# Late transposes of a stage's last token tile, and one-column inverse-root steps as tensor-scalar operations, in an fp32 two-block transformer

## The chip, the cores and the metric

One NeuronCore of a Trainium2 chip runs one program. The metric is the device time of one execution in microseconds (us). The engines are TensorE (PE in the profile; PEld is its weight load), VectorE (DVE), ScalarE (ACT), GpSimd (POOL) and SyncE (SP, which issues most DMAs).

## What is computed

Two transformer blocks in fp32 on one sequence of 512 tokens of width 1024. The first block adds three gated branches (gated linear attention, attention over 128 selected keys, cross attention to 256 memory tokens). The second has layer A (mLSTM with memory attention, then a feed-forward part of width 2816) and layer B (sliding-window attention with memory attention, then a feed-forward part). Each sublayer ends and the next begins in the same way, and this is what the change is about:

```python
def rmsnorm_2(x, g):
    y = x * lax.rsqrt(jnp.mean(x * x, axis=-1, keepdims=True) + EPS)
    return y * g

def swiglu(h, w_in, w_out):
    gate, up = jnp.split(h @ w_in, 2, axis=-1)
    return (jax.nn.silu(gate) * up) @ w_out

x = x + rmsnorm_2(y @ w, g_post)     # end of a sublayer
h = rmsnorm_2(x, g_pre)              # start of the next one
```

## The kernel before

**Products.** An fp32 product is made exact enough from three passes: each operand is split into a high part (rounded by ACT) and a low part (the difference). `mm3` (L373 to L375) issues high x high, low x high and high x low into one PSUM bank. The 512 tokens are four token tiles of 128 rows. Weights are streamed as items of [128, 1024]: SP loads an item (`load_more`, L302), ACT makes the high part (L336), DVE or POOL the low part (L337, in two pieces of 512 columns). `ctl["lo"] = POOL` gives the low parts to POOL at the end of each sublayer and in the first units of the feed-forward part. Some weights are multiplied by a gain on POOL first (L310). In the names, `h_` and `l_` stand ahead of the weight's key: `ag0`, `au0` are gate and up item 0 of layer A's feed-forward part, `ay` its down weights, `bmk`, `bmv` the memory keys and values of layer B, `kvk`, `kvv` its shared keys and values.

**Memory.** Every large tile lies in a slot of 4 KB per partition. `get` takes the slot that has been free longest, `put` (and `drop`) returns one, so the order of frees decides which tile a load has to wait for. PSUM has two banks `mm`, three `a` and three `t`.

**End of a sublayer.** `close_sublayer` (for `wo`, `awo` and `bwo`) multiplies token tile after token tile by the output weights. For tile t it then runs `residual` (sum of squares on ACT L1106, z = y * gain L1107, inverse root, x update L1113) and `prenorm` (squares L1115, inverse root, hn L1130 or, without a gain, L1128). `to_T` transposes hn on PE (L497, 8 transposes) and evicts them as high part by ACT (L502) and low part by DVE (L503). The transposes of tile t - 1 stand behind the products of tile t, those of tile 3 in a fifth turn behind the loop, so that the next stage's products follow them in the program. A scheduler then orders each engine's instructions, so the code's order is not quite the order on the engines.

**Next stage.** Behind `awo` and `bwo` the feed-forward part starts with `units_half`: five items g0, u0, g1, u1, g2, first their products with tokens 0 to 255 (tiles 0 and 1), then with tokens 256 to 511 (tiles 2 and 3). A half item is 24 matmuls of 256 columns. Behind layer A's feed-forward part `mem_kv` makes keys (mk0, mk1) and values (mv) of the memory, which need no token tile, and then come kvk and kvv, which do.

**Inverse root.** `rsqrt` with one value per row (n = 1) is a chain of one-column DVE operations: the first guess L450, then L455, L462, L463, L455, L465, L466. All but L450 and L465 read two or three tensors of [128, 1]:

```python
V.scalar_tensor_tensor(t, y_, v, y_, op0=OP.mult, op1=OP.mult)                     # L455
V.scalar_tensor_tensor(t, t, -10.0 / 3.0, t, op0=OP.add, op1=OP.mult)              # L462
V.scalar_tensor_tensor(y, t, 5.0, g, op0=OP.add, op1=OP.mult)                      # L463
V.tensor_scalar(t, t, -0.5 * 0.375 ** 3, 1.5 * 0.375, op0=OP.mult, op1=OP.add)     # L465
V.tensor_tensor(y, y, t, op=OP.mult)                                               # L466
```

Of the kernel before, what the change touches and what calls it, by code (L numbers as in the profile page):

```python
# [20 lines left out]
D = 1024  # L21
# [8 lines left out]
# column offsets of w_in  # L30
# [76 lines left out]
    # ---- second block, layer A  # L107
# [8 lines left out]
    # ---- layer B  # L116
# [10 lines left out]
def pack_weights(inp):  # L127
    """lays the weight matrices out item after item, a partition's data in one run"""
# [26 lines left out]
# ---------------------------------------------------------------- constants (of shapes alone)  # L155
# [49 lines left out]
def model_kernel(ctx: ExitStack, tc: tile.TileContext, A, out):  # L205
# [11 lines left out]
    # ------------------------------------------------------------ memory: slots of 4 KB a partition  # L217
# [43 lines left out]
    # ------------------------------------------------------------ side streams  # L261
# [19 lines left out]
    # ------------------------------------------------------------ weights  # L281
# [89 lines left out]
    # ------------------------------------------------------------ products  # L371
# [5 lines left out]
    class Act:  # L377
        """transposed activations [feature, token] as exact high and low parts"""
# [25 lines left out]
    def unit_T(key, act, ntok=512):  # L404
        """128 columns, transposed: [128 columns, tokens]"""
# [21 lines left out]
    def units_N(key, act, nt, post, bank=ps_mm):  # L427
        """256 columns, token tile by token tile: [128 tokens, 256]"""
# [13 lines left out]
    # ------------------------------------------------------------ norms  # L442
    def rsqrt(ss, n, scale, name):
        """(ss * scale + EPS) ** -0.5; ss ** -0.5 without a scale"""
# [20 lines left out]
        V.tensor_scalar(t, t, -0.5 * 0.375 ** 3, 1.5 * 0.375, op0=OP.mult, op1=OP.add)  # L465
# [26 lines left out]
    def to_T(hn, act, tt, keep=False):  # L492
        """transposes the rows of token tile tt and splits them"""
        for j in range(2):
            pt = ps_t([128, 4, 128])
# [31 lines left out]
    def head_product(o, st, j, tk, kh, kl):  # L527
        """o = q k^T; kh, kl: high and low part of the keys, in both halves (kl: at least in half j)"""
# [19 lines left out]
    def add_max(dst, src, mask, first, mx):  # L548
        """dst = src + mask; mx = max(first, dst)"""
# [7 lines left out]
    # ============================================================ start  # L557
# [20 lines left out]
    # the memory tokens enter the products without their norm, which the results are scaled by  # L578
# [66 lines left out]
    # --- keys and values of the memory of block 1  # L645
# [25 lines left out]
    # --- index keys, index weights, low-rank gate input  # L671
# [19 lines left out]
    # --- GLA gates: cumulative log decay per chunk of 64 (before the 1/16), two heads a tile  # L691
# [35 lines left out]
    # --- index queries  # L727
# [6 lines left out]
    # --- the choice of the 128 keys with the largest scores  # L734
# [36 lines left out]
    # --- cross attention, head by head  # L771
# [38 lines left out]
    def silu_gate(z, src, scale, act, k):  # L810
        """act[k] = src * scale * z * (1 + tanh(z / 2)); z in PSUM"""
# [29 lines left out]
    # --- DSA operands  # L841
# [80 lines left out]
    # --- branches: merged += 2 sigmoid(gates) * (y @ w_out)  # L922
# [24 lines left out]
    # --- GLA operands  # L947
# [105 lines left out]
    # --- DSA output gate and branch  # L1053
# [10 lines left out]
    # --- GLA output gate and branch  # L1064
# [35 lines left out]
    def residual(y, t, g, cols=HALVES, more=True):  # L1100
        """x += rmsnorm(y) * g for token tile t; y: its banks"""
# [19 lines left out]
    def prenorm(t, sx, g):  # L1121
        """the normalised rows of token tile t; without g their gain is left to the weights"""
# [10 lines left out]
    def close_sublayer(key, act, gpost, g, a):  # L1133
        """x += rmsnorm(act^T @ w) * gpost, then the transposed normalised activations a of the next sublayer"""
# [3 lines left out]
        prev = None  # L1138
        for t in range(5):
            if t < 4:  # L1140
                cols = HALVES if t < 3 else LAST
                y = [(ps_a if t % 2 else ps_mm)() for _ in cols]
                for n, sl in enumerate(cols):
                    for k in range(8):
                        mm3(y[n][:, :sl.stop - sl.start], act.hi(k)[:, 128 * t:128 * t + 128], act.lo(k)[:, 128 * t:128 * t + 128],
                            ws[k].hi[:, 0, sl], ws[k].lo[:, 0, sl], k == 0, k == 7)
# [528 lines left out]
```

## Time and profile before

| | |
|---|---|
| time, median of 3 runs | 2102.74 us (2099.51 to 2103.94) |
| span of the profiled execution | 2097.9 us |
| PE busy in it | 2038.2 us, 97% |
| DVE, ACT, POOL busy | 1102.7, 810.8, 259.0 us |

The profiled execution has no time of its own beside its span; the span lies 4.8 us under the median of the runs. All times inside the program below are counted from the span's start.

### The profile page before, as it was taken

Reading aid. Unit: us, or ns where it says so; the run is one execution under the profiler, and the core shown is the slowest. Engines: PE = TensorE matmul, PEld = TensorE weight load, DVE = VectorE, ACT = ScalarE, POOL = GpSimd, SP = SyncE. Lnnn points to the kernel's source line nnn. Section 1 sums busy time; section 2 is a strip of 40 time slices with the busy share of each in tenths; the row PEclk is TensorE's granted clock in tenths of the full one; section 3 lists DMA queues with packets and bytes.
Section 4 is the critical chain, followed back from the end, with each engine's and each line's share of the span. In section 5 each row is a group of like instructions: output and inputs, shape, how many; then the busy total and the mean of one; then the engine's idle time right before and its main releaser. Section 6 shows DMA issues by size and latency. Waiting matters only on the chain.

```text
span 2097.9 us, 26836 instructions
## 1 busy us (share of the span) xinstructions
PE 2038.2 (97%) x10234; PEld 1686.3 (80%) x10234; DVE 1102.7 (53%) x2455; ACT 810.8 (39%) x1787; POOL 259.0 (12%) x211
## 2 busy tenths in 40 slices
PE   6999999999999999999998999999989989999998
PEld 6888778879777888898877888888876778888887
DVE  8744896354654343762677443342757774333423
ACT  4533443344423242453544333232435743223311
POOL 7201100000111111000022111102220031111000
PEclk9999999999999999999999999999999999999999
DMA  6321131222222243141124222244111232312421
GB/s 260 114 71 51 56 118 61 81 81 71 81 71 82 90 141 113 69 155 60 54 78 151 67 89 81 81 152 126 60 49 38 76 116 70 111 56 81 135 81 41
DMA packets 54528, 189.57 MB, mean 90 GB/s; under 512 B 6648, under 2 KB 8832, under 8 KB 54400
## 3 DMA queue, kind: packets, MB, share of 16 engines
q1 hardware_dynamic: 52640, 185.36, 26.8%
q0 software_dynamic: 464, 1.44, 0.3%
q8 instruction: 80, 1.31, 0.2%
q10 hardware_dynamic: 1296, 1.07, 0.2%
q14 instruction: 48, 0.39, 0.1%
HBM read 185.73 MB, written 2.11 MB: 90 GB/s over the span
## 4 chain that ended last, share of the span: by engine, by line
PE 90%; DVE 6%; issue 1%; ACT 1%; DMA 1%; SPq 0%; DVEq 0%; ACTq 0%
PE mm L373 21%; PE mm L375 21%; PE mm L374 21%; PE pa L373 4%; PE pa L375 4%; PE pa L374 4%; PE pa L530 2%; PE pt L375 1%; PE pt L373 1%; PE pt L374 1%; PE pa L529 1%; PE pt L497 1%; DVE rst L455 1%; PE pa L880 1%; PE pt L1432 1%
## 5 line engine op out<-in xcount | busy, mean ns | idle before, releaser
L509 POOL TENSOR_TENSOR ffal<-t,ffah 128x512 fp32r<-128x512 f32 x44 | 61.2, 1390 | 421.1 <-ACT ffah L508 421.1
L1250 DVE SCALAR_TENSOR_TENSOR t<-t,mm 128x512 f32<-128x512 f32 x42 | 28.8, 685 | 82.5 <-PE mm L375 82.5
L497 PE MATMUL pt<-ident,hn 128*128 128x128 f32 x192 | 31.7, 304 | 36.7 <-DVE hn L1130 20.3
L374 PE MATMUL mm<-hTl,h_au 128*128 128x512 f32 (+1 forms) x176 | 66.8, 379 | 0.0
L373 PE MATMUL mm<-hTh,h_au 128*128 128x512 f32 (+1 forms) x176 | 66.8, 379 | 0.0
L373 PE MATMUL mm<-hTh,h_bu 128*128 128x512 f32 (+1 forms) x176 | 66.8, 379 | 0.0
L374 PE MATMUL mm<-hTl,h_bu 128*128 128x512 f32 (+1 forms) x176 | 66.8, 379 | 0.0
L375 PE MATMUL mm<-hTh,l_au 128*128 128x512 f32 (+1 forms) x176 | 66.8, 379 | 0.0
L375 PE MATMUL mm<-hTh,l_bu 128*128 128x512 f32 (+1 forms) x176 | 66.8, 379 | 0.0
L373 PE MATMUL mm<-hTh,h_ag 128*128 128x512 f32 (+1 forms) x168 | 63.8, 380 | 0.0
L374 PE MATMUL mm<-hTl,h_ag 128*128 128x512 f32 (+1 forms) x168 | 63.8, 380 | 0.0
L375 PE MATMUL mm<-hTh,l_ag 128*128 128x512 f32 (+1 forms) x168 | 63.7, 379 | 0.0
L373 PE MATMUL mm<-hTh,h_bg 128*128 128x512 f32 (+1 forms) x168 | 63.7, 379 | 0.0
L374 PE MATMUL mm<-hTl,h_bg 128*128 128x512 f32 (+1 forms) x168 | 63.7, 379 | 0.0
L375 PE MATMUL mm<-hTh,l_bg 128*128 128x512 f32 (+1 forms) x168 | 63.6, 379 | 0.0
L1247 ACT ACTIVATE t<-mm 128x512 f32<-128x512 f32 x40 | 23.7, 593 | 95.7 <-PE mm L375 95.7
L497 PEld LDWEIGHTS pt<-ident,hn 128*128 128x128 f32 x192 | 24.0, 155 | 42.2 <-issue 29.1
L1248 DVE SCALAR_TENSOR_TENSOR t<-t,mm 128x512 f32<-128x512 f32 x40 | 27.3, 683 | 57.7 <-ACT t L1247 57.7
L508 ACT ACTIVATE ffah<-t 128x512 fp32r<-128x512 f32 x44 | 27.5, 624 | 73.7 <-DVE t L1250 73.6
L337 DVE TENSOR_TENSOR l_ay<-w_ay,h_ay 128x512 fp32r<-128x512 f32 x44 | 30.1, 731 | 45.5 <-ACT h_ay L336 33.9
L337 DVE TENSOR_TENSOR l_bu<-w_bu,h_bu 128x512 fp32r<-128x512 f32 x38 | 25.6, 690 | 49.2 <-PE mm L374 21.3
L337 DVE TENSOR_TENSOR l_by<-w_by,h_by 128x512 fp32r<-128x512 f32 x44 | 29.2, 712 | 37.0 <-ACT h_by L336 23.2
(943 smaller groups left out, 6596.3 us busy)
## 6 DMA issues: line engine op xcount, KB each, us to landing
w_ag<-in_wpk SPq DMA_DIRECT2D x22, 512.0 KB, 3.9
w_au<-in_wpk SPq DMA_DIRECT2D x22, 512.0 KB, 3.6
w_ay<-in_wpk SPq DMA_DIRECT2D x22, 512.0 KB, 3.7
w_bu<-in_wpk SPq DMA_DIRECT2D x22, 512.0 KB, 3.5
w_bg<-in_wpk SPq DMA_DIRECT2D x22, 512.0 KB, 3.6
w_by<-in_wpk SPq DMA_DIRECT2D x22, 512.0 KB, 3.6
x<-in_x SPq DMA_DIRECT2D x8, 512.0 KB, 6.4
w_mk<-in_wpk SPq DMA_DIRECT2D x8, 512.0 KB, 6.1
```

The source lines that it names most:

```text
L337: (ctl["lo"] or V).tensor_tensor(l, s, f(h), op=OP.subtract)
L373: PE.matmul(o, lh, rh, start=first, stop=False)
L374: PE.matmul(o, lh, rl, start=False, stop=False)
L375: PE.matmul(o, ll, rh, start=False, stop=last)
L455: V.scalar_tensor_tensor(t, y_, v, y_, op0=OP.mult, op1=OP.mult)
L497: PE.transpose(pt[:, k], hn[:, 512 * j + 128 * k:512 * j + 128 * k + 128], ident)
L508: ACT.activation(h, src, AF.Copy)
L509: POOL.tensor_tensor(l, src, f(h), op=OP.subtract)
L530: PE.matmul(o, st[64 * j:64 * j + 64, j, tk], kl[64 * j:64 * j + 64], start=False, stop=True)
L1247: ACT.activation(t, og, AF.Tanh, scale=0.5)
L1248: V.scalar_tensor_tensor(t, t, 1.0, og, op0=OP.add, op1=OP.mult)
L1250: V.scalar_tensor_tensor(t, t, 0.5, ou, op0=OP.mult, op1=OP.mult)
```

## The change

Three things are changed; lines that only lose a comment are left out. First, `close_sublayer` and `ffn` no longer issue the transposes of tile 3 (in `ffn`: tiles 2 and 3). They return them as a function `late`, which the next stage calls: `units_half` ahead of its last item's first half, `mem_kv` behind its first tile of values. Second, the down product of `ffn` takes its PSUM banks in another order and transposes each tile into the banks that held its products, and kvk is made as two whole items of 512 columns instead of two half items. Third, `rsqrt` with n = 1 and `sums` are written with tensor-scalar operations, whose second and third operands are per-row scalars.

```diff
     def rsqrt(ss, n, scale, name):
...
+        if n == 1:
+            t, t1, w, w1 = [sm(1, f"rs{c}") for c in "abcd"]
+            V.tensor_scalar(t, g, v, g, op0=OP.mult, op1=OP.mult)
+            V.tensor_scalar(t1, t, -10.0 / 3.0, t, op0=OP.add, op1=OP.mult)
+            V.tensor_scalar(y, t1, 5.0, g, op0=OP.add, op1=OP.mult)
+            V.tensor_scalar(w, y, v, y, op0=OP.mult, op1=OP.mult)
+            V.tensor_scalar(w1, w, a, b, op0=OP.mult, op1=OP.add)
+            r = sm(1, "rsr")
+            V.tensor_scalar(r, y, w1, None, op0=OP.mult)
+            return r
...
     def sums(s2, n):
...
-            V.scalar_tensor_tensor(v, s2[:, i:i + 1], 1.0 / D, u, op0=OP.mult, op1=OP.add)
+            V.tensor_scalar(v, s2[:, i:i + 1], 1.0 / D, u, op0=OP.mult, op1=OP.add)
...
-    def units_half(keys, act):
+    def units_half(keys, act, late):
...
             for c, o in zip(cs, os_):
+                if t == 0 and c is cs[-1]:
+                    late()
...
     def close_sublayer(key, act, gpost, g, a):
...
-        prev = None
-        for t in range(5):
-            if t < 4:
...
-            if prev is not None:
-                to_T(prev, a, t - 1)
-            if t < 4:
-                sx = residual(y, t, gpost, cols)
-                prev = prenorm(t, sx, g)
+        for t in range(4):
...
+            if t:
+                to_T(hn, a, t - 1)
+            sx = residual(y, t, gpost, cols)
+            hn = prenorm(t, sx, g)
             pump()
+        gpost.drop()
+        g.drop()
         ctl["lo"] = None
...
+        return lambda: to_T(hn, a, 3)
...
-    def mem_kv(a, p):
+    def mem_kv(a, p, late):
...
+        def keep_v(t, o):
+            ACT.activation(v[:, t], o, AF.Copy)
+            if t == 0:
+                late()
...
-        banks = [[ps_t(), ps_t()], [ps_t(), ps_a()], [ps_a(), ps_a()], [ps_mm(), ps_mm()]]
+        pools = [[ps_mm, ps_mm], [ps_a, ps_a], [ps_a, ps_t], [ps_t, ps_t]]
+        banks = [[f_() for f_ in fs] for fs in pools]
...
+            if more and t in (1, 2):
+                to_T(rows[t - 1], nxt, t - 1, bank=pools[t - 1])
...
+        def rest():
+            for t in (2, 3):
+                to_T(rows[t], nxt, t, bank=pools[t])
...
-    o0, o1 = units_half(["kvk0", "kvk1"], hB)
-    ACT.activation(kr[:, 0], o0, AF.Copy)
-    ACT.activation(kr[:, 1], o1, AF.Copy)
     for i in range(2):
+        o = unit_T(f"kvk{i}", hB)
+        ACT.activation(kr[:, i], o, AF.Copy)
         start(s_ropek(i))
```

The order on PE behind `awo`, of before: the transposes of tile 3 (`pt<-ident,hn`) stand among the first-half products of g1 (`h_ag_9687`).

```order
L373 MATMUL pa<-hTh,h_ag_9687 128x256
L374 MATMUL pa<-hTl,h_ag_9687 128x256
L497 MATMUL pt<-ident,hn 128x128 x4
L375 MATMUL pa<-hTh,l_ag_9688 128x256
L373 MATMUL pa<-hTh,h_ag_9687 128x256
L497 MATMUL pt<-ident,hn 128x128 x4
L374 MATMUL pa<-hTl,h_ag_9687 128x256
L375 MATMUL pa<-hTh,l_ag_9688 128x256
```

The same place after the change: the transposes stand between the last first-half product of u1 (`h_au_9797`) and the first one of g2 (`h_ag_9805`).

```order
L374 MATMUL pa<-hTl,h_au_9797 128x256
L375 MATMUL pa<-hTh,l_au_9798 128x256
L510 MATMUL pt<-ident,hn 128x128 x8
L373 MATMUL pa<-hTh,h_ag_9805 128x256
L374 MATMUL pa<-hTl,h_ag_9805 128x256
L375 MATMUL pa<-hTh,l_ag_9806 128x256
```

From the end of the sublayer's products on, 62 first-half matmuls stand ahead of the transposes before, and 96 after; behind the transposes, 24 first-half matmuls (all of g2) are left where there were 58. Behind `bwo` the same rows stand with layer B's weights.

The order on ACT at that place, of before: the high parts of tile 3's transposes (`hTh<-pt`, four of them, each of two contraction tiles) and the weights around them; `h_au_10160` belongs to item u5.

```order
L502 ACTIVATE hTh<-pt 128x2x128
L336 ACTIVATE h_ag_10052<-w_ag_9748 128x512
L502 ACTIVATE hTh<-pt 128x2x128
L336 ACTIVATE h_au_10088<-w_au_9778 128x512
L502 ACTIVATE hTh<-pt 128x2x128 x2
L336 ACTIVATE h_au_10088<-w_au_9778 128x512
L336 ACTIVATE h_ag_10124<-w_ag_10020 128x512 x2
L336 ACTIVATE h_au_10160<-w_au_10058 128x512 x2
```

After the change, `h_au_10280` is the high part of item u5:

```order
L336 ACTIVATE h_ag_10244<-w_ag_10140 128x512 x2
L515 ACTIVATE hTh<-pt 128x2x128 x2
L336 ACTIVATE h_au_10280<-w_au_10178 128x512 x2
L515 ACTIVATE hTh<-pt 128x2x128 x2
L1266 ACTIVATE t_10092<-mm 128x512
```

It now stands between the two pairs of tile 3's evictions. Its item is loaded into the slot of the pre-norm gain, which is free only when DVE has made hn of tile 3 (L1130 before); before, it went to the slot of z, which L1107 frees earlier.

The order on PE ahead of the shared keys of layer B, of before: tile 3's transposes stand in the first half of kvk1 (`h_kvk_12599`).

```order
L374 MATMUL mm<-hTl,h_kvk_12597 128x256
L375 MATMUL mm<-hTh,l_kvk_12598 128x256
L373 MATMUL mm<-hTh,h_kvk_12599 128x256
L497 MATMUL pt<-ident,hn 128x128 x8
L374 MATMUL mm<-hTl,h_kvk_12599 128x256
L375 MATMUL mm<-hTh,l_kvk_12600 128x256
```

After the change they stand inside the first tile of kvv (`h_kvv.0_12848`), behind mk0, mk1 and mv, and the first products of kvk over all 512 tokens follow them:

```order
L375 MATMUL pa<-h_kvv.0_12848,hTl 128x256
L373 MATMUL pa<-h_kvv.0_12848,hTh 128x256
L374 MATMUL pa<-l_kvv.0_12849,hTh 128x256
L510 MATMUL pt<-ident,hn 128x128 x8
L373 MATMUL mm<-hTh,h_kvk_12731 128x512
L373 MATMUL mm<-hTh,h_kvk_12733 128x512
L375 MATMUL pa<-h_kvv.0_12848,hTl 128x256
```

From the first product of mk0 on, 121 matmuls stood ahead of the transposes of tile 3, and now 107; tile 2's transposes stood behind 23 matmuls and stand behind 72.

## Rows read from the trace of the kernel before

**Rows 1.** Page, busy time (1) and chain that ended last (4).

```profile
PE 2038.2 (97%) x10234; PEld 1686.3 (80%) x10234; DVE 1102.7 (53%) x2455; ACT 810.8 (39%) x1787; POOL 259.0 (12%) x211
...
PE 90%; DVE 6%; issue 1%; ACT 1%; DMA 1%; SPq 0%; DVEq 0%; ACTq 0%
```

**Rows 2.** PE's waits: us in total, times, longest us.

```profile
PE pt L497 <- DVE hn L1130: 20.3, 3, 8.9
PE pt L497 <- DVE hn L1128: 7.9, 3, 5.3
PE pt L497 <- DVE hn L489: 7.9, 5, 3.9
...
PE mm L373 <- DVE rst L465: 2.7, 1, 2.7
```

**Rows 3.** Timeline of PE behind awo: start us, us, work [idle before].

```profile
1139.89 1.08 PE L497 MATMUL pt<-ident,hn 128*128 128x128 f32 x4 [8.93 <-DVE hn L1130]
```

**Rows 4.** Timeline of DVE behind awo, token tile 3.

```profile
1123.69 1.06 DVE L1094 SCALAR_TENSOR_TENSOR ssv<-ssy,ssv 128x1 f32<-128x1 f32 x1
...
1130.00 1.03 DVE L466 TENSOR_TENSOR rsy<-rsy,rst 128x1 f32<-128x1 f32 x1
1131.06 2.38 DVE L1113 SCALAR_TENSOR_TENSOR x<-z,rsy,x 128x512 f32<-128x512 f32 x2
...
1134.92 1.21 DVE L462 SCALAR_TENSOR_TENSOR rst<-rst 128x1 f32<-128x1 f32 x1
...
1138.99 1.41 DVE L1130 SCALAR_TENSOR_TENSOR hn<-x,rsy,gain 128x512 f32<-128x512 f32 x2
1140.33 1.29 DVE L337 TENSOR_TENSOR l_au<-w_au,h_au 128x512 fp32r<-128x512 f32 x2
```

**Rows 5.** Timeline of POOL behind awo.

```profile
1130.97 1.26 POOL L337 TENSOR_TENSOR l_au<-w_au,h_au 128x512 fp32r<-128x512 f32 x1
```

**Rows 6.** DVE operations by line: ns min/median/max, forms.

```profile
L463 DVE SCALAR_TENSOR_TENSOR rsy<-rst,rsi x54: 140/159/1191, 8.8 to 2092.8; 128x1 f32<-128x1 f32 x46, 128x4 f32<-128x4 f32 x8
...
L455 DVE SCALAR_TENSOR_TENSOR rst<-rsi,ssv x36: 203/219/1028, 861.3 to 2092.3; 128x1 f32<-128x1 f32 x36
...
L465 DVE TENSOR_SCALAR rst<-rst x54: 136/154/170, 9.4 to 2093.2; 128x1 f32<-128x1 f32 x46, 128x4 f32<-128x4 f32 x8
...
L449 DVE TENSOR_SCALAR rsv<-ssg x4: 157/567/971, 564.5 to 647.0; 128x4 f32<-128x4 f32 x4
```

**Rows 7.** Stretches behind awo: each engine's busy us, PEclk granted clock.

```profile
1135.00:1140.00 5.00, 0.11 (x1) 0.14 (x2) 4.83 (x7) 2.37 (x5) 3.56 (x3) 0.50 0.37 105
1140.00:1145.00 5.00, 5.00 (x24) 5.00 (x25) 4.24 (x10) 3.61 (x9) 0.00 (x0) 0.50 0.01 2
1145.00:1150.00 5.00, 5.00 (x43) 5.00 (x42) 2.40 (x4) 1.34 (x3) 0.00 (x0) 0.98 0.72 235
```

**Rows 8.** Page, DMA issues (6): KB each, us to landing.

```profile
w_au<-in_wpk SPq DMA_DIRECT2D x22, 512.0 KB, 3.6
```

**Rows 9.** Timelines ahead of layer B's keys: PE (first row) and DVE.

```profile
1526.42 2.29 PE L497 MATMUL pt<-ident,hn 128*128 128x128 f32 x8 [5.35 <-DVE hn L1128]
...
1516.19 0.88 DVE L455 SCALAR_TENSOR_TENSOR rst<-rsi,ssv 128x1 f32<-128x1 f32 x1
...
1523.59 0.99 DVE L466 TENSOR_TENSOR rsy<-rsy,rst 128x1 f32<-128x1 f32 x1
```

**Rows 10.** Timeline of DVE at the start of the program.

```profile
36.73 0.96 DVE L462 SCALAR_TENSOR_TENSOR rst<-rst 128x1 f32<-128x1 f32 x1
...
39.91 0.77 DVE L466 TENSOR_TENSOR rsy<-rsy,rst 128x1 f32<-128x1 f32 x1
```

**Rows 11.** Start of layer B's down product: PE (two rows) and DVE.

```profile
1970.70 0.39 PE L373 MATMUL pt<-h_by,ffah 128*128 128x512 f32 x1
...
1972.06 0.39 PE L373 MATMUL pt<-h_by,ffah 128*128 128x512 f32 x1
...
1972.48 0.68 DVE L1250 SCALAR_TENSOR_TENSOR t<-t,mm 128x512 f32<-128x512 f32 x1
```

More of the change, by code (lines that the diff above doesn't have):

```diff
@@ L464, in rsqrt @@
         vyy(y)
-        V.tensor_scalar(t, t, -0.5 * 0.375 ** 3, 1.5 * 0.375, op0=OP.mult, op1=OP.add)
+        V.tensor_scalar(t, t, a, b, op0=OP.mult, op1=OP.add)
         V.tensor_tensor(y, y, t, op=OP.mult)
@@ L490, in scaled, with to_T @@
         return hn
-    def to_T(hn, act, tt, keep=False):
+    def to_T(hn, act, tt, keep=False, bank=None):
         for j in range(2):
-            pt = ps_t([128, 4, 128])
+            pt = (bank[j] if bank else ps_t)([128, 4, 128])
             for k in range(4):
@@ L1137, in close_sublayer @@
         ctl["ahead"], ctl["lo"] = 1, POOL
-        prev = None
-        for t in range(5):
-            if t < 4:
[L1141 to L1146, printed above, removed]
-                tick(2)
-                if t == 3:
-                    drop(*ws)
-                    act.drop()
-                    ctl["ahead"], ctl["stage"] = 2, 3
-            if prev is not None:
-                to_T(prev, a, t - 1)
-            if t < 4:
-                sx = residual(y, t, gpost, cols)
-                prev = prenorm(t, sx, g)
+        for t in range(4):
+            cols = HALVES if t < 3 else LAST
+            y = [(ps_a if t % 2 else ps_mm)() for _ in cols]
+            for n, sl in enumerate(cols):
+                for k in range(8):
+                    mm3(y[n][:, :sl.stop - sl.start], act.hi(k)[:, 128 * t:128 * t + 128], act.lo(k)[:, 128 * t:128 * t + 128],
+                        ws[k].hi[:, 0, sl], ws[k].lo[:, 0, sl], k == 0, k == 7)
+            tick(2)
+            if t == 3:
+                drop(*ws)
+                act.drop()
+                ctl["ahead"], ctl["stage"] = 2, 3
+            if t:
+                to_T(hn, a, t - 1)
+            sx = residual(y, t, gpost, cols)
+            hn = prenorm(t, sx, g)
             pump()
+        gpost.drop()
+        g.drop()
         ctl["lo"] = None
+        return lambda: to_T(hn, a, 3)
     def mem_prep(l):
@@ L1187, in mem_kv @@
             pump()
-        units_N(f"{p}mv", a, 2, lambda t, o: ACT.activation(v[:, t], o, AF.Copy), ps_a)
+        def keep_v(t, o):
+            ACT.activation(v[:, t], o, AF.Copy)
+            if t == 0:
+                late()
+        units_N(f"{p}mv", a, 2, keep_v, ps_a)
         a.drop()
@@ L1235, in mem_block, with ffn @@
             put(*qs, *kv)
-    def ffn(p, l, hT, more, side={}):
+    def ffn(p, l, hT, late, more, side={}):
         gpost = Gain("g_ffn_post_2", l)
@@ L1241, in ffn @@
         ctl["lo"] = POOL
-        first = units_half([f"{p}g0", f"{p}u0", f"{p}g1", f"{p}u1", f"{p}g2"], hT)
+        first = units_half([f"{p}g0", f"{p}u0", f"{p}g1", f"{p}u1", f"{p}g2"], hT, late)
         ctl["lo"] = None
@@ L1277, in ffn @@
         nxt = Act(8, "hT") if more else None
-        prev = None
-        for t in range(5):
-            if t < 4:
-                for n in range(2):
-                    for k in range(NFF - NR, NFF):
-                        step(k, ws[k - NFF + NR], banks[t][n], t, HALVES[n])
-                tick(2)
-                if t == 3:
-                    drop(*ws)
-                    for j in range((NFF - NR) // 2, NFF // 2):
-                        act.drop_group(j)
-                    ctl["ahead"], ctl["stage"] = 2, 3
-            if prev is not None:
-                to_T(prev, nxt, t - 1)
-            if t < 4:
-                sx = residual(banks[t], t, gpost, more=more)
-                if more:
-                    prev = prenorm(t, sx, None)
+        rows = []
+        for t in range(4):
+            for n in range(2):
+                for k in range(NFF - NR, NFF):
+                    step(k, ws[k - NFF + NR], banks[t][n], t, HALVES[n])
+            tick(2)
+            if t == 3:
+                drop(*ws)
+                for j in range((NFF - NR) // 2, NFF // 2):
+                    act.drop_group(j)
+                ctl["ahead"], ctl["stage"] = 2, 3
+            if more and t in (1, 2):
+                to_T(rows[t - 1], nxt, t - 1, bank=pools[t - 1])
+            sx = residual(banks[t], t, gpost, more=more)
+            if more:
+                rows.append(prenorm(t, sx, None))
         gpost.drop()
         ctl["lo"] = None
-        return nxt
+        def rest():
+            for t in (2, 3):
+                to_T(rows[t], nxt, t, bank=pools[t])
+        return nxt, rest
     def wout(key, act, gpost, gnext):
-        gp, g, a = Gain(*gpost), Gain(*gnext), Act(8, "hT")
-        close_sublayer(key, act, gp, g, a)
-        gp.drop()
-        g.drop()
-        return a
+        a = Act(8, "hT")
+        return a, close_sublayer(key, act, Gain(*gpost), Gain(*gnext), a)
     memA = mem_prep(0)
-    hA = wout("wo", mg, ("g_post",), ("g_mix_pre_2", 0))
-    kvm = mem_kv(memA, "a")
+    hA, late = wout("wo", mg, ("g_post",), ("g_mix_pre_2", 0))
+    kvm = mem_kv(memA, "a", late)
     aux = get([32, 896], F32, "aux")
@@ L1475, in model_kernel @@
     put(*hm, *sgo)
-    hF = wout("awo", mix, ("g_mix_post_2", 0), ("g_ffn_pre_2", 0))
+    hF, late = wout("awo", mix, ("g_mix_post_2", 0), ("g_ffn_pre_2", 0))
     def rotary():
@@ L1506, in model_kernel @@
     sides_a = {6: lambda: T.update(rot=rotary()), 4: lambda: T.update(mem=mem_prep(1))}
-    hB = ffn("a", 0, hF, True, sides_a)
+    hB, late = ffn("a", 0, hF, late, True, sides_a)
     cosT, sinT = T["rot"]
     memB = T["mem"]
-    kvB = mem_kv(memB, "b")
+    kvB = mem_kv(memB, "b", late)
     def rope(dst, rawt):
@@ L1633, in model_kernel @@
     put(*khd, *kld, vB, T["rt"], *qx)
-    hF = wout("bwo", mix, ("g_mix_post_2", 1), ("g_ffn_pre_2", 1))
-    ffn("b", 1, hF, False)
+    hF, late = wout("bwo", mix, ("g_mix_post_2", 1), ("g_ffn_pre_2", 1))
+    ffn("b", 1, hF, late, False)
 def build(inputs):
```

8 lines of the change are left out of this document (3 added, 5 removed).

## The prediction

> **What bounds the kernel now.** The page comes first: PE is busy for 97% of the span, and the chain of work that ended last lies on PE for 90% and on DVE for 6% [rows 1]. So TensorE sets the time, and a gain can come only from places where it stands still or runs at a lower clock. The view of PE's waits lists these places [rows 2]. Nearly all are transposes of normalised rows that wait for DVE: three waits for hn from L1130 (20.3 us in all, the longest 8.9), three for hn from L1128 (7.9, the longest 5.3), five at the start of the program (7.9). One more of 2.7 us there is a product that waits for a DVE operation of a one-column inverse root.
>
> The timeline shows the longest one: behind `awo` PE stands still for 8.93 us until 1139.89, so from 1130.96 [rows 3]. The wait behind `bwo` reads the same, and the third one of L1130, behind `wo`, is then 20.3 - 2 x 8.93 = 2.4. On DVE the reason is visible [rows 4]: the one-column operations of token tile 3 take about 1 us each, as long as a small tile's work. Their own line shows minima of 0.14 and 0.20 us [rows 6]. In that stretch POOL makes low parts back to back until 1132.2 [rows 5]. It is the operations with two tensor inputs that stretch; L465, a tensor-scalar operation, never took over 0.17 us in its 54 uses [rows 6].
>
> The granted clock shows a second loss. During the wait it falls to 0.50, the lower level of 1.2 GHz, and stays there for the 5 us after it: 24 matmuls between 1140 and 1145, then 43 in the next 5 us [rows 7]. From 1139.89 to about 1145.1 PE does half of what it could, so each long wait costs about 2.6 us more. The two places together cost 2 x (8.93 + 2.6) = 23.1 us.
>
> **Late transposes behind awo and bwo.** 96 instead of 62 first-half matmuls now precede tile 3's transposes: 34 more, each 0.12 us (43 in 5 us) [rows 7], so 4.1 us. PE reaches the transposes at 1130.96 + 4.1 = 1135.1.
>
> Would hn be there? Between 1123.69 and 1131.03 six one-column operations took 1.06, 1.02, 0.67, 1.01, 0.99 and 1.03 us (first and last in [rows 4]), in place of 0.15 to 0.22 each: 4.7 us too much. In the second root three took 1.2 us (one of them in [rows 4]), 3.1 too much. As tensor-scalar operations I price all at the 0.15 of L465 plus 0.06 for a tensor's place, by the 0.22 of L455. The trace has no such operation with two per-row scalars; the bounds are 0.15 and the slow 1.0 of the old form, and I choose the low end because L465 stood in the same busy stretch. Then x starts at 1131.06 - 4.7 = 1126.4, takes 2.4 us beside POOL [rows 4], the squares and the second root need some 2.5, and DVE now does one item's low parts (1.3) ahead of hn, which takes 1.4 to 2.4. The first half of hn is ready at 1133 to 1135, the second by 1136. Of the wait, 0.4 us may stay. With it goes the low clock.
>
> Behind the transposes only g2's first half covers their eviction: 24 matmuls, 2.9 us. ACT evicts one pair, and must then make the high part of u5 before the second pair. u5's load starts when hn is finished (1134 to 1136), lands 3.6 us later [rows 8], ACT needs 1.1 for it and about 1 us for the eviction and its low part: 1139.7 to 1141.7. PE is back from transposes and g2 at 1135.1 + 1.0 + 2.9 = 1139.0 and uses the first pair for 0.7 us more: wait 0 to 2, and more if the load is slower. I take 1.7. Each place then saves 8.93 + 2.6 - 0.4 - 1.7 = 9.4, and both 18.8.
>
> **Behind layer A's feed-forward part.** Five one-column operations between 1516.19 and 1524.58 lasted 0.66 to 0.84 us too long, 3.9 in all (first and last in [rows 9]), and POOL was multiplying gains then. hn of tile 3 comes at 1522.5 instead of 1526.4. But PE now has 107 instead of 121 matmuls ahead of it, so it waits longer and has 14 x 0.12 = 1.7 us more to do behind. The long wait and its low clock stay. kvk now needs all tokens at once, so part of the eviction is exposed, but tile 2's wait (7.9 - 5.3 = 2.6 with a small one) is covered by 49 more matmuls, 5.9 us. I count 3.9 - 1.7 = 2.2, less 0.2: 2.0, bounds +1 and -8 (all waits of [rows 2]'s second line gone).
>
> **Behind wo.** Only three or four matmuls more stand ahead of the transposes: 0.5 us of the 2.4.
>
> **Start of the program.** Nothing moves here, only the root. In the wait of 3.9 us [rows 2] four operations lost 0.8, 0.8, 0.7 and 0.6 us (first and last in [rows 10]): 3.0. The wait of 2.7 us behind L465 has slow operations ahead of it too. Weights' low parts stand between them on DVE, so I count 4.0 for the start; bounds 0 and 6.
>
> **Banks of the down product.** Its second product now takes the bank of the last up item. In layer B that bank is read until 1973.16, and PE would want it six matmuls behind 1970.70, at 1972.06 [rows 11]: a new wait of 1.1 us. In layer A the same sum gives 0.2. Cost 1.3.
>
> **Elsewhere** the one-column operations are hidden behind PE's products, and faster ones change nothing; with that cover gone a slow one costs 0.8.
>
> **The rule that speaks against it.** L449, a tensor-scalar operation on 4 columns, took up to 0.97 us, median 0.57, in one use [rows 6]. So a tensor-scalar form is not safe as such; one column is the case that never stretched. The Trainium skill says in "SBUF — State Buffer", section "Who interferes with whom", that a DVE instruction with two SBUF inputs contends with a GpSimd instruction that reads SBUF, and that tensor_scalar can enter a two-port mode and contend too. By that rule, read strictly, the new steps could stay slow, the first rival below. "DVE: scalar operands, raw-bit mode, write accounting and state across instructions", section 1, says that a per-row scalar does not take up the second tensor stream, which is the way that I take; no row here shows it for two scalars.
>
> **Sum.** 18.8 + 2.0 + 0.5 + 4.0 - 1.3 = 24.0 us, out of a span of 2097.9: 2073.9. The profiled execution lies 4.8 us under the median of the runs, and I subtract from the median: 2078.7. What tells a change from none here is about 0.2%, 4.2 us.
>
> **Rivals.** *The steps stay slow* (per-row scalars wait for POOL like tensors). For it: L449's four columns. Against it: L465. Then hn comes at 1139.9 as before, PE waits 8.93 - 4.1 = 4.8, the low clock stays, u5 lands at 1144, the second pair is out at 1146 against a need at 1144.6: each place saves 4.1 - 1.4 = 2.7, layer B's keys lose 1.7, the start gains nothing, the banks cost 1.3: 5.4 + 0.5 - 1.7 - 1.3 = 2.9, so 2099.8.
>
> *The evictions give back more.* u5's load shares the queues with others and lands 2 us later, and the second wait brings the low clock back: 2 + 2.6 more at each place, sum 24.0 - 9.2 = 14.8, 2088.
>
> *Everything comes off*: both places save 11.5, the start 6, behind wo 2.4, the keys 8, the banks cost nothing: 39, 2063. Against it: the 107 matmuls are fewer than before.
>
> *Slower.* ACT's queue is in order. If u5's load lands late, the second pair, the low parts behind it, and all second-half products stand still. This costs one us per us of lateness at two places. It decides when it eats 27 us (24.0 plus the 3.4 already counted), 13.7 at each: a landing 15 us or more behind hn, against 3.6 [rows 8]. Little speaks for it; at 15.5 us it gives about 2108.
>
> *It does not do what it says*: behind `wo` the scheduler moved the transposes by four matmuls only, but behind `awo` and `bwo` the order shows 34. No chance there beyond the first rival's.
>
> **How the numbers follow.** Forecast (2070 to 2084): 0.54. Everything off: 0.14. Evictions give back more: 0.18. Steps stay slow: 0.09. Slower: 0.05. The time is the likeliest one's, 2078.7. For eight in ten the range takes the forecast, the evictions' case and most of the way to the best: 2064 to 2092. Faster by over 0.2%: 0.54 + 0.14 + 0.18 = 0.86; within 0.2%: 0.08, most of the slow steps' case; slower: 0.06.
>
> **What will show it.** Right: one-column operations near 0.2 us beside a busy POOL; hn's waits behind `awo` and `bwo` under 1 us, with PEclk 1.00 there; a wait of about 1.7 us of a second-half product for L515 or L516, with u5's load ahead of it; some 1 us at the start of layer B's down product. Wrong: steps of 1 us; a wait of 5 us at the transposes; a clock of 0.50 behind the evictions; a long wait ahead of kvk.

## The result and the profile after

The changed kernel takes 2079.64 us (median of 4 runs, 2077.36 to 2083.1) against 2102.73 before: a ratio of 0.9896, 95% interval 0.9882 to 0.9910, 23.1 us less. The forecast was 2078.7.

The profiled execution has a span of 2081.1 us, only 16.8 less than before. At two places that the change does not touch (from 1003 and from 1641.7 us) the clock was at its lower level for longer than in the profile before, which cost about 6 us (the second one is in the last section). The other three runs are 2.7 to 5.7 us shorter, at a mean granted clock of 0.993 or 0.994 against 0.991 here. Line numbers below are those of each run's own kernel.

The page after, busy time and chain:

```profile
PE 2041.9 (98%) x10186; PEld 1682.6 (81%) x10186; DVE 1100.2 (53%) x2455; ACT 810.8 (39%) x1787; POOL 265.4 (13%) x211
...
PE 89%; DVE 7%; ACT 2%; issue 1%; DMA 1%; POOL 0%; SPq 0%; DVEq 0%; ACTq 0%
```

PE is busy for 98%, and its share of the chain stays near 90% [rows 1]. PE's waits after:

```profile
PE pa L374 <- DVE l_kvv.0_12849 L337: 5.5, 1, 5.5
PE pt L510 <- DVE hn L1143: 4.0, 5, 1.0
PE mm L374 <- DVE hTl L516: 2.8, 4, 1.3
...
PE pt L510 <- DVE hn L502: 1.8, 3, 1.3
PE mm L373 <- DVE t L1269: 1.4, 2, 1.0
```

The three waits of L1130 [rows 2] have become five of L1143, 4.0 us in all, the longest 1.05. New ones are there: for a low part of kvv's weights, for the low parts of hn's transposes (L516), and for a bank of the down product (L1269).

To see what each place gave, the end of the same PE products is taken from both traces, and the shift is followed from stage to stage. This table is worked out that way (minus is earlier, us of one profiled execution each):

| stage | forecast | after | steps alone | moves alone |
|---|---|---|---|---|
| start of the program | -4.0 | -7.7 | -5.3 | -1.1 |
| behind `wo` | -0.5 | -0.2 | -1.4 | -0.4 |
| behind `awo`, to the last up item of layer A | -9.4 | -7.2 | -4.8 | -4.0 |
| down product of layer A | +0.2 | +0.7 | +0.1 | +0.6 |
| layer B's memory keys to kvv | -2.0 | -3.2 | -0.3 | 0.0 |
| behind `bwo`, to the last up item of layer B | -9.4 | -7.1 | -4.8 | -4.4 |
| down product of layer B | +1.1 | +1.3 | 0.0 | +1.2 |

The last two columns belong to the first two experiments. The stages left out hold nothing but clock drops that move from run to run.

Behind `awo`, DVE's timeline after answers to [rows 4]:

```profile
1120.91 2.97 DVE L1126 SCALAR_TENSOR_TENSOR x<-z,rsr,x 128x512 f32<-128x512 f32 x2
...
1125.18 0.27 DVE L461 TENSOR_SCALAR rsa<-rsi,ssv 128x1 f32<-128x1 f32 x1
...
1126.48 0.21 DVE L467 TENSOR_SCALAR rsr<-rsy,rsd 128x1 f32<-128x1 f32 x1
1126.61 1.50 DVE L337 TENSOR_TENSOR l_au<-w_au,h_au 128x512 fp32r<-128x512 f32 x1
1128.03 3.45 DVE L1143 SCALAR_TENSOR_TENSOR hn<-x,rsr,gain 128x512 f32<-128x512 f32 x2
1131.41 1.76 DVE L337 TENSOR_TENSOR l_au<-w_au,h_au 128x512 fp32r<-128x512 f32 x1
1133.10 1.28 DVE L337 TENSOR_TENSOR l_ag<-w_ag,h_ag 128x512 fp32r<-128x512 f32 x2
...
1136.11 0.74 DVE L516 TENSOR_TENSOR hTl<-pt,hTh 128x256 fp32r<-128x256 f32 x2
```

The one-column steps take 0.27 and 0.21 us although POOL works without a break (13.00 of 13 us in the first row of the windows below; the busy times are PE, PEld, DVE, ACT, POOL). By line, over the whole program (minimum, median and maximum in ns):

```profile
L461 DVE TENSOR_SCALAR rsa<-rsi,ssv x36: 261/272/276, 853.6 to 2075.3; 128x1 f32<-128x1 f32 x36
...
L462 DVE TENSOR_SCALAR rsb<-rsa x46: 194/214/216, 8.2 to 2075.6; 128x1 f32<-128x1 f32 x46
```

None of them ever reached 0.3 us, where L463 went up to 1.2 [rows 6]. They are not shorter than the old ones at their best: 0.27 for two per-row scalars, 0.21 for one, against 0.22 and 0.16.

DVE's rows show where the rest went. The x update takes 2.97 us (2.38 before), one piece of u3's low part stands ahead of hn, and hn itself takes 3.45 us, where it took 1.41 in [rows 4]: it now runs while POOL does. Behind hn, one more piece of u3, g4, u4 and half of g5 (left out in part) fill DVE until L516 at 1136.11. The windows there:

```profile
1116.00:1129.00 13.00, 13.00 (x111) 12.92 (x109) 10.35 (x26) 11.07 (x26) 13.00 (x10) 1.00 0.79 318
...
1134.00:1139.00 5.00, 3.39 (x26) 2.98 (x25) 4.11 (x9) 1.87 (x4) 0.00 (x0) 1.00 0.92 320
```

PE's timeline at the transposes and at the second half's first products:

```profile
1129.96 0.63 PE L510 MATMUL pt<-ident,hn 128*128 128x128 f32 x4 [0.83 <-DVE hn L1143]
1131.63 0.63 PE L510 MATMUL pt<-ident,hn 128*128 128x128 f32 x4 [1.05 <-DVE hn L1143]
...
1134.97 0.28 PE L373 MATMUL mm<-hTh,h_ag 128*128 128x256 f32 x1
1136.57 0.39 PE L374 MATMUL mm<-hTl,h_ag 128*128 128x256 f32 x1 [1.32 <-DVE hTl L516]
```

ACT's timeline, with u5's high part ahead of the second pair of evictions:

```profile
1135.08 1.15 ACT L336 ACTIVATE h_au<-w_au 128x512 fp32r<-128x512 f32 x2 [2.40 <-DMA w_au<-in_wpk]
1136.55 0.72 ACT L515 ACTIVATE hTh<-pt 128x256 fp32r<-128x256 f32 x2 [0.32 <-DVE hTl L516]
```

PE comes to the transposes at 1129.1, waits 0.83 and 1.05 us for the halves of hn, and at the second-half products 1.32 us for L516 and 0.29 once more. PEclk stays at 1.00, against 0.50 in [rows 7].

Behind `bwo` hn's waits are the same (0.87 and 1.04), but there the clock did fall: it was at 0.50 for 3.4 us from 1720.2, right behind them (the figure behind POOL's busy time is PEclk, 0.57 over these 4 us).

```profile
1720.00:1724.00 4.00, 3.73 (x19) 3.77 (x20) 4.00 (x6) 0.66 (x2) 1.25 (x1) 0.57 0.61 204
```

PE then came later to the second-half products and waited only 0.29 us for them, so that this place gives as much as the other.

### The profile page after: what moved, and what is told of

It is laid out like the page before. It is cut to its first block, busy times and chain, and to the rows that moved or that the text cites. A ratio compares the mean times of both kernels' runs of the same rounds, so it can differ in the third digit from the quotient of the medians.

```text
span 2081.1 us, 26742 instructions
## 1 busy us (share of the span) xinstructions
PE 2041.9 (98%) x10186; PEld 1682.6 (81%) x10186; DVE 1100.2 (53%) x2455; ACT 810.8 (39%) x1787; POOL 265.4 (13%) x211
## 4 chain that ended last, share of the span: by engine, by line
PE 89%; DVE 7%; ACT 2%; issue 1%; DMA 1%; POOL 0%; SPq 0%; DVEq 0%; ACTq 0%
PE mm L373 21%; PE mm L374 21%; PE mm L375 21%; PE pa L373 3%; PE pa L375 3%; PE pa L374 3%; PE pa L543 2%; PE pt L374 1%; PE pt L373 1%; PE pt L375 1%; PE pa L542 1%; PE pa L893 1%; PE pt L1452 1%; PE pa L1016 1%; PE pa L1605 1%
## 5 line engine op out<-in xcount | busy, mean ns | idle before, releaser
L1269 DVE SCALAR_TENSOR_TENSOR t<-t,mm 128x512 f32<-128x512 f32 x42 | 28.8, 685 | 82.5 <-PE mm L375 82.5
L1120 DVE TENSOR_TENSOR z<-mm,gain 128x512 f32<-128x512 f32 x16 | 11.0, 689 | 73.3 <-ACT t L1119 73.3
L952 POOL TENSOR_TENSOR merged<-merged,t 128x512 f32<-128x512 f32 x16 | 25.5, 1592 | 165.7 <-DVE t L950 165.7
```

Source lines behind the costliest of these rows:

```text
L952: POOL.tensor_tensor(m, m, t, op=OP.add)
L1269: V.scalar_tensor_tensor(t, t, 0.5, ou, op0=OP.mult, op1=OP.mult)
```

## The experiments

Two theories stood against each other on the whole change. One: two-tensor operations on DVE stretch beside POOL, and the new form does not, so steps and moves both count. The other: the moves carry the gain. On the wait behind the transposes stood the forecast's reason (u5's load) against DVE's queue.

**The steps alone** (the kernel before with the new `rsqrt` and `sums`).

```diff
+            V.tensor_scalar(t, g, v, g, op0=OP.mult, op1=OP.mult)
...
+            V.tensor_scalar(v, s2[:, i:i + 1], 1.0 / D, u, op0=OP.mult, op1=OP.add)
```

> The kernel before with only the inverse root and the sums written as tensor-scalar operations; no transposes move. Theory (two-tensor steps stretch beside POOL, tensor-scalar ones do not, and a stall ends when hn is ready): the start gains the 7.7 us that the changed kernel's trace shows there; behind awo and bwo PE still arrives early, the wait falls from 8.9 to about 6 us and the clock still drops, 3 us each; ahead of layer B's keys some 4 us; nothing is lost at the down product's banks. Sum 18, so about 2085 us (2080 to 2089). Rival (the moved transposes carry the gain and the steps matter at the start only): about 2095 us. In the trace: steps of 0.2 us beside a POOL that is as busy as before.

Measured: 2084.82 us (6 runs), ratio 0.9915 (0.9900 to 0.9930). With hn earlier, the wait behind `awo` is this:

```profile
1127.51 1.09 PE L507 MATMUL pt<-ident,hn 128*128 128x128 f32 x4 [3.45 <-DVE hn L1140]
...
1129.18 1.08 PE L507 MATMUL pt<-ident,hn 128*128 128x128 f32 x4 [0.38 <-DVE hn L1140]
```

8.93 has become 3.45 and 0.38, with the clock drop still behind it. The steps are the larger half of the change, 17.5 of its 23 us, and not at the start only. The sum came out as expected, its parts did not: 5.3 at the start for 7.7, 4.8 at each of the two places for 3, and 0.3 ahead of layer B's keys for 4.

**The moves alone** (the changed kernel with the old `rsqrt` and `sums`; the diff is the reverse of the one above).

> The changed kernel with the inverse root and the sums as they were; all moved transposes, banks and kvk items stay. Theory (steps of 1 us keep hn late, so the extra 4.1 us of products cover only part of the wait): hn's waits behind awo and bwo stay near 5 us with the clock drop, the start gains nothing, the banks cost 1.3: about 2099 us (2095 to 2103), less than 5 us better than before. Rival (the moves alone carry most of the gain): about 2088 us. If the two parts simply added up, this and the run with the steps alone would together gain the 23 us of the whole change.

Measured: 2097.37 us (12 runs), ratio 0.9977 (0.9965 to 0.9988), 5 us less. On DVE behind `awo` a step and hn read:

```profile
1133.71 1.22 DVE L465 SCALAR_TENSOR_TENSOR rst<-rst 128x1 f32<-128x1 f32 x1
...
1137.80 1.42 DVE L1133 SCALAR_TENSOR_TENSOR hn<-x,rsy,gain 128x512 f32<-128x512 f32 x2
```

And PE at the transposes:

```profile
1138.70 1.94 PE L500 MATMUL pt<-ident,hn 128*128 128x128 f32 x8 [4.92 <-DVE hn L1133]
```

The steps take 1.2 us, and of the 8.93 only the 4.0 us that the 34 products cover are gone. The two gains, 17.5 and 5, add up to about the whole in the runs. In the table they don't: behind `awo` 4.8 and 4.0 would make 8.8, and the change has 7.2. The 1.6 us between them are as much as the waits for L516 there (1.32 and 0.29), which neither run has.

**u5's load in another slot.** The gain is returned with the late transposes, so u5 gets a slot that is free early.

```diff
         gpost.drop()
-        g.drop()
...
-        return lambda: to_T(hn, a, 3)
+        def late():
+            g.drop()
+            to_T(hn, a, 3)
...
+        return late
```

> The changed kernel with the pre-norm gain returned at the late transposes instead of at the sublayer's end: item u5 is loaded into a slot that POOL frees early, so that ACT never waits for its load between the two pairs of evictions; the order on ACT and DVE stays the same. Theory of the prediction (the second pair of evictions waits for u5's load): the waits of second-half products behind awo and bwo (1.32 and 0.29 us at the first place in the changed kernel) go, 3 us in all: about 2076.5 us. Rival (the low parts of the evictions stand behind seven pieces of weights on DVE, which is busy without a break from hn to them): waits of 1.3 us stay, 2079.6 us within 1.5.

Measured: 2077.31 us (4 runs), ratio 0.9881 (0.9861 to 0.9900), an interval that overlaps the changed kernel's. The median lies between the two expectations, nearer to that of the prediction's theory, and decides nothing; the trace does. ACT behind `awo`:

```profile
1129.34 1.14 ACT L336 ACTIVATE h_au<-w_au 128x512 fp32r<-128x512 f32 x2
1133.32 0.71 ACT L515 ACTIVATE hTh<-pt 128x256 fp32r<-128x256 f32 x2 [2.83 <-DVE hTl L516]
```

DVE from the end of hn on:

```profile
1128.18 1.76 DVE L337 TENSOR_TENSOR l_au<-w_au,h_au 128x512 fp32r<-128x512 f32 x1
...
1132.87 0.74 DVE L516 TENSOR_TENSOR hTl<-pt,hTh 128x256 fp32r<-128x256 f32 x2
```

ACT now makes u5's high part at once, and still waits 2.83 us ahead of the second pair of evictions, for L516. On DVE, L516 comes 4.69 us behind hn's end (1128.18 to 1132.87); in the changed kernel it is 4.70 (1131.41 to 1136.11). The stage gives 7.1, as in the changed kernel. PE's own wait there is shorter (0.29 in all, instead of 1.32 and 0.29), as behind `bwo` above: the clock was at 0.50 for 3.4 us in this execution and PE came later. The load of u5 is not the cause; DVE's queue is what is left, and the next run tests it.

**Three more items' low parts on POOL** (u3, g4, u4), which takes them out of DVE's queue.

```diff
         first = units_half([f"{p}g0", f"{p}u0", f"{p}g1", f"{p}u1", f"{p}g2"], hT, late)
-        ctl["lo"] = None
         for i in range(NFF):
+            if i == 4:
+                ctl["lo"] = None
```

> The changed kernel with POOL making the low parts of three more items (u3, g4, u4) at the start of both feed-forward parts, so that DVE has two pieces of weights instead of seven ahead of tile 3's low parts, and none ahead of hn. Rival of the prediction (DVE's backlog makes the second-half products wait): their waits go and hn comes some 1.5 us earlier, 3 us per place, 6 in all: about 2074 us. Theory of the prediction (u5's load is what they wait for): only hn's waits shrink, about 2077 us. Against both: POOL works longer and hn, which took 3.45 us beside it, stays slow: 2079 us.

Measured: 2070.64 us (5 runs), ratio 0.9855 (0.9834 to 0.9876). DVE behind `awo`, from the last step on:

```profile
1122.81 0.21 DVE L467 TENSOR_SCALAR rsr<-rsy,rsd 128x1 f32<-128x1 f32 x1
1123.06 3.09 DVE L1143 SCALAR_TENSOR_TENSOR hn<-x,rsr,gain 128x512 f32<-128x512 f32 x2
1126.08 3.47 DVE L337 TENSOR_TENSOR l_ag<-w_ag,h_ag 128x512 fp32r<-128x512 f32 x2
1129.47 0.74 DVE L516 TENSOR_TENSOR hTl<-pt,hTh 128x256 fp32r<-128x256 f32 x2
```

hn follows its root at once, and L516 comes 3.4 us behind hn's end. Behind `awo` and `bwo` the table's figures are -10.0 and -10.2, and no PE wait over 0.45 is left there. This shows the backlog as the cause. The two places give 5.9 us more than in the changed kernel, as expected; the median is 9.0 lower, and the rest does not come from them. hn stays slow (3.09), as POOL is still busy.

**The transposes one half item earlier** (ahead of u1).

```diff
-                if t == 0 and c is cs[-1]:
+                if t == 0 and c is cs[-2]:
```

> The changed kernel with the late transposes ahead of the last but one half item (u1) instead of the last (g2) behind awo and bwo: 24 matmuls, 2.9 us, less in front and more behind. Theory (the place is a trade: in front PE waits for hn, behind it for the evictions that stand behind DVE's weights): hn's waits rise from 1.9 to some 4.8 us per place and bring the low clock back, the evictions' wait (up to 1.6) goes: 1.3 to 4 us slower per place, about 2084 us. Rival (hn is nearly ready anyway and the cover behind is what lacks): about 2077 us.

Measured: 2083.03 us (4 runs), ratio 0.9911 (0.9894 to 0.9928). PE at the transposes behind `awo`:

```profile
1128.43 1.09 PE L510 MATMUL pt<-ident,hn 128*128 128x128 f32 x4 [3.45 <-DVE hn L1143]
...
1130.10 1.09 PE L510 MATMUL pt<-ident,hn 128*128 128x128 f32 x4 [0.37 <-DVE hn L1143]
```

The wait in front grows to 3.45 and 0.37, the low clock is back, and behind there is none. The places give 4.9 each, as with the steps alone. The trade is as stated, and the change's place is the better one.

**The banks of the down product.**

```diff
-        pools = [[ps_mm, ps_mm], [ps_a, ps_a], [ps_a, ps_t], [ps_t, ps_t]]
+        pools = [[ps_a, ps_a], [ps_mm, ps_mm], [ps_a, ps_t], [ps_t, ps_t]]
```

> The changed kernel with the two mm banks taken by the second token tile of the down product instead of the first. Theory (the first products wait for DVE to read the last up item out of its bank): the waits of 0.35 and 1.02 us at the start of the down products go, 1.4 to 2.0 us in all: about 2078 us. Rival (DVE reads that bank late in any order and the wait only moves to a later product): 2079.6 us, no change.

Measured: 2075.11 us (4 runs), ratio 0.9873 (0.9858 to 0.9888). In the stages: +0.1 and +0.7 in place of +0.7 and +1.3, so 1.2 us come from the banks. The medians are 4.5 apart, but the intervals of the two ratios overlap, and the rest has no place in the trace.

**Three parts together** (low parts on POOL, the slot, the banks).

> Three parts together on the changed kernel: POOL makes three more items' low parts, u5 gets the early slot, and the mm banks go to the second token tile. Theory (DVE's backlog was the wait behind awo and bwo; the slot is worth nothing beside it; the banks 1.4 to 2.0): about 2069 us. Rival (the slot is worth 2 of its own): about 2067 us. Rival (parts overlap and nothing is added to the first): 2070.6 us.

Measured: 2076.79 us (4 runs), ratio 0.9883 (0.9868 to 0.9897): worse than the low parts alone. The miss is visible on DVE behind `awo`:

```profile
1131.02 3.43 DVE L337 TENSOR_TENSOR l_ag<-w_ag,h_ag 128x512 fp32r<-128x512 f32 x2 [2.43 <-POOL l_ag L337]
1134.37 1.62 DVE L516 TENSOR_TENSOR hTl<-pt,hTh 128x256 fp32r<-128x256 f32 x4
```

g5's low part waits 2.43 us, by the profile for POOL, and L516 behind it in the queue makes PE wait 2.50. The shifted slot put a dependence on POOL's pieces into DVE's queue: the next run, without it, has no such wait. Through which tile is not shown.

**Low parts and banks, without the slot.**

> POOL makes three more items' low parts and the mm banks go to the second token tile; the gain's slot is returned as in the changed kernel. Theory (in the run with the slot as well, DVE stood 2.4 us behind POOL ahead of tile 3's low parts; without the slot's shift that wait goes, and the two other parts add up): 2070.6 less 1.3 to 2.0: about 2069 us. Rival (the banks' run and this one overlap): 2070.6 us.

Measured: 2072.57 us (4 runs), ratio 0.9863 (0.9843 to 0.9883). The stages add up (-10.1 and -10.0 behind `awo` and `bwo`, +0.1 and +0.5 at the banks); the time cannot be told from 2070.64.

**The kernel before, with no low parts on POOL.** All three places that set `ctl["lo"]` to POOL set None.

```diff
-        ctl["ahead"], ctl["lo"] = 1, POOL
+        ctl["ahead"], ctl["lo"] = 1, None
...
-        ctl["lo"] = POOL
+        ctl["lo"] = None
...
-        ctl["ahead"], ctl["lo"], ctl["stage"] = 3, POOL, 4 if more else 2
+        ctl["ahead"], ctl["lo"], ctl["stage"] = 3, None, 4 if more else 2
```

> The kernel before, with DVE instead of POOL making the low parts at the ends of sublayers and in the first units; the inverse root stays in its old form. Theory (the one-column steps with two tensors stretch because POOL works beside them): the steps behind awo and bwo take 0.14 to 0.22 us each instead of 1.0 to 1.2, though DVE is busier. What is won there, some 8 to 10 us, goes to the pieces that DVE now makes itself (12 of 0.69 us, 8.2), so the time stays near 2102 us (2096 to 2110). Rival (the steps stretch for another reason, their short form or the neighbours in the queue): steps of 1 us remain and the time rises by 10 us or more.

Measured: 2081.40 us (4 runs), ratio 0.9905 (0.9890 to 0.9920). The steps did what was expected, the time did not: it is 20.7 us better, with the old steps and the old place of the transposes. DVE behind `awo`:

```profile
1136.36 0.16 DVE L462 SCALAR_TENSOR_TENSOR rst<-rst 128x1 f32<-128x1 f32 x1
1136.56 0.16 DVE L463 SCALAR_TENSOR_TENSOR rsy<-rst,rsi 128x1 f32<-128x1 f32 x1
...
1138.37 1.41 DVE L1130 SCALAR_TENSOR_TENSOR hn<-x,rsy,gain 128x512 f32<-128x512 f32 x2
```

PE there:

```profile
1139.26 0.63 PE L497 MATMUL pt<-ident,hn 128*128 128x128 f32 x4 [1.13 <-DVE hn L1130]
```

The old steps take 0.16 us, and hn 1.41. Moving 12 pieces costs DVE less than the stretched operations had cost it, so hn is ready 7.8 us sooner against PE. Behind `awo` and `bwo` this gives 10.1 and 10.9; the start, where POOL still multiplies by gains, gives nothing.

**The same with the new steps** (no transposes moved).

> The kernel before with the inverse root as tensor-scalar operations and with all low parts on DVE; no transposes move. Theory (behind awo and bwo the stall came from POOL beside DVE, and with POOL gone neither the steps' form nor the late transposes matter there; the steps' form still matters at the start, where POOL multiplies weights by gains): 2081.4 less 5.4 to 7.7 at the start: about 2075 us. Rival (the steps' form is worth as much as in the run with the steps alone, 17 us): below 2068 us.

Measured: 2071.93 us (4 runs), ratio 0.9865 (0.9848 to 0.9881). Start -5.4, behind `awo` and `bwo` -10.8 each: the steps gain at the start only, as stated; the median lies 3 us under the 2075 expected.

**The change with no low parts on POOL.**

> The changed kernel with all low parts on DVE. Theory (hn and x are no longer stretched by POOL, and the pieces that DVE now makes stand ahead of hn, not between hn and its low parts): behind awo and bwo 10 to 11 us each in place of the changed kernel's 7.2, so about 2073 us. Rival (12 more pieces on DVE make hn or its low parts later than POOL did, so waits of 3 us or more at each place): 2080 us or more.

Measured: 2075.04 us (4 runs), ratio 0.9882 (0.9863 to 0.9902). DVE behind `awo`, in the second root:

```profile
1127.08 0.68 DVE L337 TENSOR_TENSOR l_au<-w_au,h_au 128x512 fp32r<-128x512 f32 x1
...
1129.62 1.41 DVE L1143 SCALAR_TENSOR_TENSOR hn<-x,rsr,gain 128x512 f32<-128x512 f32 x2
```

PE there:

```profile
1130.51 1.29 PE L510 MATMUL pt<-ident,hn 128*128 128x128 f32 x8 [2.04 <-DVE hn L1143]
```

Now a piece of 0.68 us stands between most steps of the root and the next, hn comes late, and PE waits 2.04 us even at the late place. The stages give 8.9 and 7.6 (at the second the clock was low for 3.4 us), against 10.8 each with the transposes at their old place. With POOL out of the way, the late transposes have nothing left to win there.

**The same with the banks, and the copies of the memory keys on ACT.**

```diff
-                V.tensor_copy(kh[64 - 64 * j:128 - 64 * j, 2 * u + j], f(kh[s, 2 * u + j]))
+                ACT.activation(kh[64 - 64 * j:128 - 64 * j, 2 * u + j], f(kh[s, 2 * u + j]), AF.Copy)
```

> As the run before this one, with the mm banks at the second token tile and with ACT instead of DVE copying the memory keys into the other half of the partitions. Theory (ahead of layer B's keys DVE is busy without a break, and each of its operations taken away there moves the end; four copies take 1.7 us): 1.3 to 2.0 for the banks and 1.7 for the copies, 3 to 4 us less than the run before. Rival (ACT's copies wait behind ACT's weights, or the wait there is set by a load): 1.3 to 2.0 less.

Measured: 2074.64 us (4 runs), ratio 0.9882 (0.9863 to 0.9901): no gain. The banks' stages are at +0.1 and +0.4, but layer B's keys give 2.1 instead of 3.2. PE's waits there:

```profile
PE pa L374 <- DVE l_kvv.1_12885 L337: 1.9, 2, 1.5
PE pt L510 <- DVE hn L1141: 1.8, 1, 1.8
PE mm L374 <- DVE hTl L516: 1.3, 1, 1.3
```

The order changed with the copies, and the wait of 5.5 us for kvv's low part broke up into three others. What bounds that stage stays open.

## Why the prediction held, and where its steps did not

- **The steps as tensor-scalar operations**: right. Chosen at 0.15 to 0.21, they took 0.21 to 0.27 beside a busy POOL, and the bound of 1.0 did not occur. The first rival (the steps stay slow) falls. By the Trainium skill, "SBUF — State Buffer", section "Who interferes with whom", a DVE instruction with two SBUF inputs contends with a GpSimd instruction that reads SBUF; the trace agrees, with 1.21 us for L462 beside POOL [rows 4] and 0.16 without it. "DVE: scalar operands, raw-bit mode, write accounting and state across instructions" of the Trainium skill, section 1, says of per-row scalars (a bf16 scale or an int32 index) that they do not take up the second tensor stream; the 0.276 us that L461, in fp32, takes at most agrees. The rows of before also show why an old step took about 1 us. L462 of [rows 4] ends at 1136.13, and the piece that POOL began just ahead of it ends at 1136.12; every slow step of the two roots ends like this, within 0.02 us behind a piece of POOL. One slow step passes per piece:

```profile
1134.85 1.27 POOL L337 TENSOR_TENSOR l_au<-w_au,h_au 128x512 fp32r<-128x512 f32 x1 [2.62 <-ACT h_au L336]
```

- **Behind `awo` and `bwo`**: 7.2 and 7.1 in place of 9.4. PE came to the transposes 4.1 us later, as stated. The term for hn, 0.4, was too small: 1.9, since hn itself ran beside POOL (3.45) behind a piece of u3. The term for the evictions, 1.7, was right in size (1.32 and 0.29), but its reason was wrong: DVE's queue, not u5's load. That leaves 8.0, and most of the last 0.8 is in the stops, which cost more than their idle time: the two products at 1134.97 and 1136.57 start 1.60 us apart, where such products follow each other every 0.12, so 1.48 are lost for a wait of 1.32. The four stops behind `awo` lose 4.2 us in this way for 3.5 of waiting. "With it goes the low clock" held behind `awo` and not behind `bwo`.
- **Start**: 7.7 in place of 4.0, above its bound of 6; the other ten runs with the new steps gave 4.9 to 8.1. The term counted 3.0 off the longest wait for hn and 1.0 elsewhere. In fact the waits for hn of L489 [rows 2] fell from 7.9 to 1.8 us in all (L502 after; 1.4 and 1.3 of these lie near 850 us, not at the start). And it left out the clock, which was low there for 10.2 us before and for 3.4 after. In the six runs of the ten where it was low for 6.8 us the start gave 4.9 to 6.0, in the other four, with 3.4 or none, 6.3 to 8.1.
- **Layer B's keys**: 3.2 in place of 2.0, and not by the sum that was made: the 3.9 that it puts down to the steps are not there, since steps alone give 0.3 and moves alone nothing. With the steps alone, DVE's pieces of weights fill the time between the shorter steps, and PE waits 8.8 us for hn there, where it waited 7.9 [rows 2]. DVE's timeline of that run:

```profile
1509.07 0.14 DVE L462 TENSOR_SCALAR rsd<-rsc 128x1 f32<-128x1 f32 x1
1509.13 1.46 DVE L337 TENSOR_TENSOR l_bmq<-w_bmq,h_bmq 128x512 fp32r<-128x512 f32 x1
1510.52 0.20 DVE L464 TENSOR_SCALAR rsr<-rsy,rsd 128x1 f32<-128x1 f32 x1
```

After the whole change the long wait is for kvv's low part (5.5), which DVE makes between the last steps of tile 3's root and hn:

```profile
1505.83 0.95 DVE L337 TENSOR_TENSOR l_kvv.0_12849<-w_kvv.0_12347,h_kvv.0_12848 128x512 fp32r<-128x512 f32 x1
...
1508.15 2.44 DVE L1141 TENSOR_SCALAR hn<-x,rsr 128x512 f32<-128x512 f32 x2
```

The clock is low at that place for 6.8 us, before it was for 10.2 in two parts; what else makes up the 3.2 stays open. This hn is itself a tensor-scalar operation, on 512 columns, and takes 1.2 us a piece beside POOL, which multiplies gains then; the same one before (L1128) took from 0.48 to 1.35. So the form alone does not protect an operation; one column did.

- **Behind `wo`** 0.2, with 0.5 forecast. **Banks**: 2.0 us, with 1.3 forecast.

The errors of the two large terms, 4.5 us too high together, and of the start, 3.7 too low, nearly cancel. The mechanism was right (steps free of POOL, and products that cover the rest of the wait); that the sum came within 1 us of the time is luck.

## What to carry to other kernels

When one-column operations take seven times their minimum, look at the engine beside them before their place in the order: giving POOL less to do won 20.7 us here, nearly as much as the whole change. Shorter steps help only where nothing else is put between them. A moved stall is followed by the next queue: ahead of a late transpose look at what stands between it and its low parts on DVE. The best versions here keep POOL or DVE free at that place: 2070.64 and 2071.93 us (ratios 0.9855 and 0.9865, where the change has 0.9896), each faster than both kernels, and not to be told apart.

## Not expected of the hardware

In the changed kernel's profile the clock was at its lower level for 10.2 us from 1641.7, and PE had no wait over 0.25 us ahead of it. PEclk is the first figure behind POOL's busy time; 10.2 of 15 us at 0.50 make the 0.66:

```profile
1640.00:1655.00 15.00, 15.00 (x67) 9.72 (x65) 6.87 (x40) 7.00 (x28) 0.00 (x0) 0.66 0.03 3
```

It cost 4.3 us of that execution. Two other traces (the moves alone, the kernel before without POOL) show the same 10.2 us near that place, and the rest less or none. Its cause stays open.

A second thing: hn (L1130) took 742 to 754 ns in all its 24 uses before, and L1143 takes 745 to 1781 after. The operation is the same; what POOL does at that time is not, and in the kernel before without low parts on POOL it takes 743 to 754.
